# A hybrid decoder layer on one core: the second norm's gain moved from w_up's columns to the rows, and its row factor moved up in GpSimd's order

## The chip, the cores and the metric

One Trainium2 chip, of which the program uses one core. TensorE (PE) multiplies and transposes; VectorE (DVE), ScalarE (ACT) and GpSimd (POOL) do the elementwise work; SyncE (SP) issues the transfers. Each engine runs its own instructions in the order in which they stand, and an instruction that waits holds everything behind it on that engine. The metric is the device time of one execution in microseconds.

## The reference

One layer on 1024 tokens with 16 learned rows in front of them; width 1024, hidden width 4096, everything in float32.

```python
h = concatenate([meta, x])
hn = rms_norm(h, norm1_gain)
q, k, v, u = split(hn @ w_in)
h = h + concatenate([diff_attention(q, k, v, ...), conformer_conv(u, ...)]) @ w_out
hn = rms_norm(h, norm2_gain)
a = relu(hn @ w_up)
h = h + (a * a) @ w_down
return h[n_meta:]

def rms_norm(x, g):
    return x * rsqrt(mean(x * x) + EPS) * g
```

The change concerns the second `rms_norm` and what feeds `hn @ w_up`.

## The kernel before

**Numbers.** Every float32 operand of a product is held as a high and a low part, and each product is three matmuls (`three`: high by high at line 319, high by low at 320, low by high at 321). A pair is made by `halves` (lines 806 to 809): ACT copies the high part (L808), DVE or POOL subtracts it for the low part (L809).

**Stages.** First norm, input projection and convolution run to about 225 us; then keys, queries, values and attention, with `w_out`'s products mixed in, to about 475; then the second norm and the first products of `w_up`; the up-projection to about 824; the down-projection to the end.

**Second norm.** `attn_out(t, nh)` adds half a row tile of attention's result to the convolution's (L693, DVE) and squares it on ACT with the sums kept (`ssq`, L695). When both halves of a tile are there, two small POOL instructions make the factor `rs2` of its 128 rows (L698 `ms`, L699 the power, shown as `rs`). `normed(t)` multiplies the rows by it (L832, `xn`, two instructions per row tile), PE transposes them (L835, `htr`), and `norm_first` (tiles 7 to 4, read back from DRAM as `h2t`), `norm_second` (tiles 3 to 0, kept in SBUF as `h2k`) and `norm_third` make the operands from the transposed tiles. The last row tile is t = 0. The norm's gain is not in `xn`: it is multiplied into w_up's rows.

**Up-projection.** It is done in 16 groups of 256 columns by Strassen and Winograd's scheme of seven products; `up_product(g, n)` is one of them. Products 1 to 3 use rows as they are (`hn`), products 4 to 7 use sums of them (`hnt`: "t4", "t1", "t2", "t3"). `wload` fetches half of a group's columns into one of four buffers `wr` (L890) and scales it by the gain: for the early groups, in tiles of 128 columns, in one POOL instruction (L892); for all others in four ACT instructions per tile (L894). `up_prep` then makes the sums `s1`, `s2` on DVE and the pairs `wp`. `up_early` does products 1 and 2 of groups 0 to 3 as soon as the rows are there. In a later group, product 6 adds to product 1 in the same PSUM tile `px`, and ACT snaps the result into `sn` (L941) before product 7 may add to `px`.

**Order.** Nothing of the order is written by hand but a few marks: a list scheduler with simulated times sets each engine's order, and `tc.high_priority()` lifts what stands under it. Buffers come from pools: 4 of `wr` (which `h2t` uses too), 6 of `wp`, 7 of `ut` (`h2k`), 6 PSUM banks that `po`, `htr`, `px`, `py`, `pz` and `pw` share.

**Start.** SP loads the first rows, weights and small vectors one after the other; the convolution's taps `cw` are among them (L223), and `gains` [128, 2, 8] holds both norms' gains with the channel on the partition.

Of the kernel before, what the change touches and what calls it, by code (L numbers as in the profile page):

```python
# [16 lines left out]
P = 128  # L17
# [42 lines left out]
def hybrid_layer_kernel(  # L60
# [36 lines left out]
    def small(shape, name, bufs=2):  # L97
        return sp.tile(shape, F32, tag=name, name=name, bufs=bufs)
# [59 lines left out]

    xm = cp.tile([P, 8, 48], F32R, tag="xm", name="xm")
    G.memset(xm.bitcast(F32), 0.0)
    mraw = slot([NMETA, D], F32, "mraw")
    nc.sync.dma_start(mraw, meta)
# [62 lines left out]
    V.tensor_scalar(lnh[:, 1, :], cvec[:, :, 2], 0.5, None, ALU.mult)  # L227
    gsub = cp.tile([P, 1], F32, tag="gsub", name="gsub")
    V.tensor_scalar(gsub, cvec[:, 0, 3:4], (1.0 - 0.2) * P ** 0.5, None, ALU.mult)

    gq = tmp([P, HD], F32, "gq")
    gk = tmp([P, HD], F32, "gk")
# [451 lines left out]
    def attn_out(pool, t, nh, keep=None):  # L684

        if keep is None:
            hs = tmp([P, 512], F32, "hs")
        else:
            hs = keep.tile([P, 512], F32, tag="ut", name="h2k", bufs=UT)
            h2t.setdefault(t, []).append(hs)  # L690
        nc.sync.dma_start(hs, cvo[t, nh])
        ps = half_out(pool, ma, state[0, nh], t)
        V.tensor_tensor(out=hs, in0=hs, in1=ps, op=ALU.add)  # L693
        nc.sync.dma_start(h2d[t][:, 512 * nh:512 * nh + 512], hs)
        S.activation(ps, hs, AF.Square, scale=D ** -0.5, accum_out=ssq[:, t, nh:nh + 1])  # L695
        if nh:
            ms = small([P, 8], "ms", 4)[:, :1]
            G.tensor_scalar(ms, ssq[:, t, 0:1], ssq[:, t, 1:2], EPS, ALU.add, ALU.add)  # L698
            G.tensor_tensor(out=rs2[:, t:t + 1], in0=ms, in1=mhalf[:, :1], op=ALU.pow)  # L699

    uqs, pend = [], []
    for t in range(NT):
# [48 lines left out]
    for n in range(-1, len(units) + BLAG):  # L751
        if n < 0:
            with tc.high_priority(offset=PRI):
                for f, *a in fill_at.get(n, []):
                    f(*a)
            continue
        if n != 1:
            ahead(n)
        if n == 0 and APOSN[1] >= NT:
            for j in range(4):  # L760
                conv_act(1, j)
        if n < len(units):
            mixed.append(mix(*units[n], *pend.pop(0)))
        if n == 1:
            st_pool.__exit__(None, None, None)
            yt_pool.__exit__(None, None, None)
            aux_pool = tc.tile_pool(name="aux", bufs=1, side="right", reuse_waits="tile")
            aux = aux_pool.__enter__()
            ap2 = tc.tile_pool(name="ap2", bufs=2, reuse_waits="tile")
            late_pools["pt"] = ap2.__enter__()  # L770
            ahead(1)
        if n >= BLAG:
            i, h = units[n - BLAG]
            values(i, h, mixed.pop(0))
            if h == NH - 1:
                done.append((n + FIN, i, state["osb"], state["oss"]))
            if done and (n >= done[0][0] or n - BLAG == len(units) - 1):
                finish(*done.pop(0)[1:])
        with tc.high_priority(offset=PRI):
            for f, *a in fill_at.get(n, []):  # L780
                f(*a)
# [39 lines left out]
    def normed(t):  # L821

        if t in h2t:
            hv = h2t[t]
        else:
            h2 = up.tile([P, D], F32, tag="wr", name="h2t", bufs=WRB)
            nc.sync.dma_start(h2, h2d[t])
            hv = h2[:, :512], h2[:, 512:]
        banks = []
        for kf in range(2):  # L830
            xn = sp.tile([P, 512], F32, tag="raw", name="xn", bufs=4)
            V.tensor_scalar(xn, hv[kf], rs2[:, t:t + 1], None, ALU.mult)  # L832
            bank = pcm.tile([P, 4, P], F32, tag="mm", name="htr")
            for q in range(4):
                T.transpose(bank[:, q, :], xn[:, q * P:(q + 1) * P], ident)  # L835
            banks.append(bank)
        return banks
# [29 lines left out]
    def norm_third():  # L867

        for name in ("t4", "t1", "t3"):
            operand(name)  # L870
            for c in (256, 0):
# [3 lines left out]
                if name == "t4":  # L875
                    sub(V, r21, t2, r21)
                    halves(hi, lo, r21)
                elif name == "t1":
                    halves(hi, lo, t1)
                else:  # L880
                    sub(V, t2, t2, r11)
                    halves(hi, lo, t2)
# [4 lines left out]
    def wload(g, j, n):  # L887

        r = up.tile([P, 4, n], F32, tag="wr", name="wr", bufs=WRB, padded_shape=[P, 4, 256])
        nc.sync.dma_start(r, w_up[512 * j:512 * j + 512, 256 * g:256 * g + n].rearrange("(k p) f -> p k f", p=P))  # L890
        if n == P:
            G.tensor_tensor(out=r, in0=r, in1=gains[:, 1, 4 * j:4 * j + 4].unsqueeze(2).broadcast_to([P, 4, P]), op=ALU.mult)  # L892
        for k in range(4) if n > P else ():
            S.activation(r[:, k, :], r[:, k, :], AF.Copy, scale=gains[:, 1, 4 * j + k:4 * j + k + 1])  # L894
        return r

    def wpair(g, n, v, eng=None):
# [199 lines left out]
            next(run[g])  # L1097
    next(run[NG - 1])
    up_pool.__exit__(None, None, None)
    ps_c.__exit__(None, None, None)  # L1100
    tr_pool.__exit__(None, None, None)

# [134 lines left out]
```

## Time and profile before

| | |
|---|---|
| median of 3 runs | 1135.59 us (1133.06 to 1140.71) |
| profiled execution | 1135.33 us, of which 1133.2 is the traced span |
| PE busy | 1098.8 us, 97% of the span |
| DVE, ACT, POOL busy | 817.2, 617.1 and 149.2 us |
| mean granted clock of PE | 0.995 of full speed |

A busy share is an average over stages. An engine at 97% leaves some 34 us in which it waited; whether another engine's work matters is read at those waits. A granted clock of 1.00 is PE's full 2.4 GHz, 0.50 its lower level of 1.2 GHz.

### The profile page before, as it was taken

How to read it: one execution, taken by the hardware profiler on the slowest of the kernel's cores; microseconds unless marked ns; L12 is line 12 of the kernel's file. 1: busy time of each engine (PE TensorE's matmuls, PEld its weight loads, DVE VectorE, ACT ScalarE, POOL GpSimd, SP SyncE). 2: the span in 40 equal slices, each digit the busy share in tenths (PEclk: the TensorE clock that was granted, in tenths of full speed). 3: DMA queues.
4: the chain of work that ended last, by engine and by line, in shares of the span. 5: the costliest groups of instructions: out<-in, count | busy, mean ns of one | idle time of the engine just before them, and what ended most of it. 6: DMA issues, size and time to landing. Idle time of an engine off the chain costs nothing.

```text
span 1133.2 us, 15762 instructions
## 1 busy us (share of the span) xinstructions
PE 1098.8 (97%) x5696; PEld 925.5 (82%) x5696; DVE 817.2 (72%) x1354; ACT 617.1 (54%) x1378; POOL 149.2 (13%) x160
## 2 busy tenths in 40 slices
PE   6999999999999999898999999999999999999998
PEld 6999788877788887786888877888878888888887
DVE  7699899977888788689688868787656545356340
ACT  7521465447667677568767667767555333323320
POOL 3000564313001351261000000000000000000000
PEclk9999999999999999998999999999999999999999
DMA  7420011100213411365489989879399675565600
GB/s 266 121 76 1 1 38 38 29 10 19 75 66 103 131 66 66 122 224 170 154 309 330 323 277 343 320 251 339 125 336 380 251 258 212 197 227 201 221 38 37
DMA packets 89309, 191.23 MB, mean 169 GB/s; under 512 B 7552, under 2 KB 28288, under 8 KB 83600
## 3 DMA queue, kind: packets, MB, share of 16 engines
q1 hardware_dynamic: 89232, 190.24, 48.0%
q8 instruction: 44, 0.72, 0.3%
q14 instruction: 33, 0.27, 0.1%
HBM read 130.44 MB, written 59.77 MB: 168 GB/s over the span
## 4 chain that ended last, share of the span: by engine, by line
PE 72%; DVE 10%; DMA 8%; ACT 5%; issue 3%; POOL 1%; SPq 0%; DVEq 0%; ACTq 0%; POOLq 0%
PE py L319 6%; PE py L320 6%; PE py L321 6%; PE px L321 5%; PE px L319 5%; PE px L320 5%; DMA wr<-in_w_up 3%; PE pu L319 3%; PE pu L320 3%; PE pu L321 3%; DMA wdr<-in_w_down 3%; PE pq L320 3%; PE pq L319 3%; PE pq L321 3%; PE ops L620 2%
## 5 line engine op out<-in xcount | busy, mean ns | idle before, releaser
L809 DVE TENSOR_TENSOR pair<-rv,pair 128x2048 fp32r<-128x2048 f32 x56 | 127.0, 2289 | 112.0 <-ACT pair L808 111.8
L808 ACT ACTIVATE pair<-rv 128x2048 fp32r<-128x2048 f32 x56 | 105.2, 1911 | 163.2 <-PE py L321 77.9
L319 PE MATMUL py<-pair 128*128 128x512 f32 x256 | 99.6, 389 | 0.0
L320 PE MATMUL py<-pair 128*128 128x512 f32 x256 | 99.6, 389 | 0.0
L321 PE MATMUL py<-pair 128*128 128x512 f32 x256 | 99.6, 389 | 0.0
L319 PE MATMUL px<-pair 128*128 128x512 f32 x192 | 74.8, 390 | 1.0 <-ACT pair L808 1.0
L320 PE MATMUL px<-pair 128*128 128x512 f32 x192 | 74.7, 389 | 0.0
L321 PE MATMUL px<-pair 128*128 128x512 f32 x192 | 73.8, 390 | 0.2 <-DVE pair L809 0.2
L320 PE MATMUL pu<-xT,w 128*128 128x260 f32 x256 | 72.4, 286 | 0.0
L321 PE MATMUL pu<-xT,w 128*128 128x260 f32 x256 | 71.7, 285 | 0.0
L319 PE MATMUL pu<-xT,w 128*128 128x260 f32 x256 | 71.7, 286 | 0.0
L894 ACT ACTIVATE wr<-wr,gains 128x256 f32<-128x256 f32 x128 | 55.0, 498 | 30.6 <-DMA wr<-in_w_up 29.7
L945 ACT ACTIVATE a<-a 128x512 f32<-128x512 f32 x60 | 36.9, 626 | 35.9 <-DVE a L812 24.6
L321 PEld LDWEIGHTS py<-pair 128*128 128x128 f32 x256 | 48.1, 188 | 10.0
L319 PEld LDWEIGHTS py<-pair 128*128 128x128 f32 x256 | 48.1, 188 | 9.9
L320 PEld LDWEIGHTS py<-pair 128*128 128x128 f32 x256 | 48.1, 188 | 9.9
L319 PE MATMUL px<-hnt,wp 128*128 128x512 f32 x128 | 50.5, 395 | 3.9 <-ACT sn L941 3.9
L321 PE MATMUL pq<-w,xT 128*128 128x512 f32 x128 | 50.9, 398 | 0.0
L319 PE MATMUL pq<-w,xT 128*128 128x512 f32 x128 | 50.9, 397 | 0.0
L320 PE MATMUL pq<-w,xT 128*128 128x512 f32 x128 | 50.8, 397 | 0.0
L320 PE MATMUL px<-hnt,wp 128*128 128x512 f32 x128 | 50.4, 394 | 0.4 <-DVE hnt L809 0.4
L321 PE MATMUL px<-hnt,wp 128*128 128x512 f32 x128 | 50.5, 394 | 0.0
(301 smaller groups left out, 3197.6 us busy)
## 6 DMA issues: line engine op xcount, KB each, us to landing
rv<-as SPq DMA_DIRECT2D x28, 1024.0 KB, 6.3
wr<-in_w_up SPq DMA_DIRECT2D x32, 512.0 KB, 5.2
as<-a SPq DMA_DIRECT2D x64, 256.0 KB, 5.4
wdr<-in_w_down SPq DMA_DIRECT2D x8, 2048.0 KB, 9.5
ws<-wdr SPq DMA_DIRECT2D x32, 512.0 KB, 4.5
rv<-ws SPq DMA_DIRECT2D x16, 1024.0 KB, 4.8
as<-as SPq DMA_DIRECT2D x48, 256.0 KB, 4.1
rv<-in_w_down SPq DMA_DIRECT2D x12, 1024.0 KB, 6.6
```

What stands on the lines that cost most here:

```text
L319: T.matmul(ps, st[0], mv[0], start=first, stop=False, skip_group_check=more)
L320: T.matmul(ps, st[0], mv[1], start=False, stop=False, skip_group_check=more)
L321: T.matmul(ps, st[1], mv[0], start=False, stop=last, skip_group_check=more)
L620: T.matmul(ops, u[:, 0, b, :], vb.rearrange("p a e -> p (a e)"), start=b == 0, stop=False)
L808: S.activation(hi, src, AF.Copy)
L809: (eng or V).tensor_tensor(out=lo, in0=src, in1=hi.bitcast(F32), op=ALU.subtract)
L894: S.activation(r[:, k, :], r[:, k, :], AF.Copy, scale=gains[:, 1, 4 * j + k:4 * j + k + 1])
L945: S.activation(c, c, AF.Relu)
```

## The change

**Gain.** `wload` no longer scales: the POOL multiply (L892) and the four ACT scales per tile (L894) are gone. In their place `xn` is made by one instruction that multiplies the rows by their factor and by the gain, which must then lie along the row: `gain2` is a tile [128, 1024] with the gain repeated on every partition. It comes by two transfers: one at the start writes the 1024 gains into a row `grow` in DRAM, 4 bytes each, behind the taps on SP; one within attention broadcasts that row to all partitions (512 KB). Its space is found by moving `xm` to another pool.

**Order.** The two POOL instructions of `rs2` are marked high priority. The low parts of operand "t1" in `norm_third` go to POOL.

```diff
-    xm = cp.tile([P, 8, 48], F32R, tag="xm", name="xm")
+    xm = wpool[0].tile([P, 8, 48], F32R, tag="xm", name="xm", bufs=1)
...
+    grow = dr.tile([8, P], F32, tag="grow", name="grow")
+    nc.sync.dma_start(grow.rearrange("k p -> p k"), gains[:, 1, :])
...
         if nh:
-            ms = small([P, 8], "ms", 4)[:, :1]
-            G.tensor_scalar(ms, ssq[:, t, 0:1], ssq[:, t, 1:2], EPS, ALU.add, ALU.add)
-            G.tensor_tensor(out=rs2[:, t:t + 1], in0=ms, in1=mhalf[:, :1], op=ALU.pow)
+            with tc.high_priority():
+                ms = small([P, 8], "ms", 4)[:, :1]
+                G.tensor_scalar(ms, ssq[:, t, 0:1], ssq[:, t, 1:2], EPS, ALU.add, ALU.add)
+                G.tensor_tensor(out=rs2[:, t:t + 1], in0=ms, in1=mhalf[:, :1], op=ALU.pow)
...
+            gain_pool = tc.tile_pool(name="gain", bufs=1, side="right", reuse_waits="tile")
+            gain2 = gain_pool.__enter__().tile([P, D], F32, tag="gain2", name="gain2")
+            nc.sync.dma_start(gain2, grow.rearrange("k p -> (k p)").partition_broadcast(P))
...
-            V.tensor_scalar(xn, hv[kf], rs2[:, t:t + 1], None, ALU.mult)
+            V.scalar_tensor_tensor(xn, hv[kf], rs2[:, t:t + 1], gain2[:, 512 * kf:512 * kf + 512], ALU.mult, ALU.mult)
...
-                    halves(hi, lo, t1)
+                    halves(hi, lo, t1, G)
...
-        if n == P:
-            G.tensor_tensor(out=r, in0=r, in1=gains[:, 1, 4 * j:4 * j + 4].unsqueeze(2).broadcast_to([P, 4, P]), op=ALU.mult)
-        for k in range(4) if n > P else ():
-            S.activation(r[:, k, :], r[:, k, :], AF.Copy, scale=gains[:, 1, 4 * j + k:4 * j + k + 1])
```

In the new kernel the lines behind the additions have moved: the low part is L817, `xn` L840, the rows' factor L703 and L704, the squares L699, `sn` L945, the load of `wr` L898.

The order of POOL from the low parts of the first early tiles on, before; the lines with `rs` are the factors of row tiles 1 and 0:

```order
L809 TENSOR_TENSOR wp<-wr,wp 128x512 x4
L698 TENSOR_SCALAR ms<-ssq 128x1
L892 TENSOR_TENSOR wr<-wr,gains 128x4x128 x2
L699 TENSOR_TENSOR rs_2665<-ms,mhalf 128x1
L892 TENSOR_TENSOR wr<-wr,gains 128x4x128 x2
L809 TENSOR_TENSOR wp<-wr,wp 128x512 x2
L698 TENSOR_SCALAR ms<-ssq 128x1
L809 TENSOR_TENSOR wp<-wr,wp 128x512
L699 TENSOR_TENSOR rs_2665<-ms,mhalf 128x1
L809 TENSOR_TENSOR wp<-wr,wp 128x512
```

And now; the first `rs` is row tile 2's, and the two that follow each other behind the four `wp` are those of tiles 1 and 0:

```order
L817 TENSOR_TENSOR wp<-wr,wp 128x512 x2
L703 TENSOR_SCALAR ms<-ssq 128x1
L704 TENSOR_TENSOR rs_2667<-ms,mhalf 128x1
L817 TENSOR_TENSOR wp<-wr,wp 128x512 x4
L703 TENSOR_SCALAR ms<-ssq 128x1
L704 TENSOR_TENSOR rs_2667<-ms,mhalf 128x1
L703 TENSOR_SCALAR ms<-ssq 128x1
L704 TENSOR_TENSOR rs_2667<-ms,mhalf 128x1
L817 TENSOR_TENSOR wp<-wr,wp 128x512 x2
L817 TENSOR_TENSOR hnt_6502<-scr,hnt_6502 128x4x256 x2
```

The multiplies of `wr` are gone, both last factors stand together ahead of the last two `wp`, and operand "t1"'s low parts (`hnt`) stand at the end.

The order of DVE from row tile 1's last sum to row tile 0's `xn`, before:

```order
L693 TENSOR_TENSOR h2k<-h2k,po 128x512
L832 TENSOR_SCALAR xn<-h2k,rs_2665 128x512 x2
L812 TENSOR_TENSOR scr<-htr,hraw 128x4x128
L812 TENSOR_TENSOR scr<-htr,scr 128x4x128
L812 TENSOR_TENSOR hraw<-scr,hraw 128x4x256
L809 TENSOR_TENSOR hnt_6195<-scr,hnt_6195 128x4x128
L809 TENSOR_TENSOR hn_6196<-htr,hn_6196 128x4x128
L812 TENSOR_TENSOR scr<-scr,hraw 128x4x256
L812 TENSOR_TENSOR scr<-htr,hraw 128x4x128
L832 TENSOR_SCALAR xn<-h2k,rs_2665 128x512 x2
```

And now, from row tile 1's `xn` to the release of its PSUM banks:

```order
L840 SCALAR_TENSOR_TENSOR xn<-h2k,rs_2667,gain_3418 128x512 x2
L697 TENSOR_TENSOR h2k<-h2k,po 128x512
L823 TENSOR_TENSOR s_6367<-wr 128x512
L820 TENSOR_TENSOR s_6368<-s_6367,wr 128x512
L820 TENSOR_TENSOR wr<-wr 128x4x128
L820 TENSOR_TENSOR scr<-htr,hraw 128x4x128
L840 SCALAR_TENSOR_TENSOR xn<-h2k,rs_2667,gain_3418 128x512 x2
L820 TENSOR_TENSOR scr<-htr,scr 128x4x128
L820 TENSOR_TENSOR hraw<-scr,hraw 128x4x256
L817 TENSOR_TENSOR hnt_6198<-scr,hnt_6198 128x4x128
L820 TENSOR_TENSOR scr<-htr,hraw 128x4x128
L817 TENSOR_TENSOR hn_6199<-htr,hn_6199 128x4x128
```

Three instructions that read a full group's `wr` (`s`, `s`, `wr`) now stand ahead of row tile 0's `xn`, and four that read row tile 1's transposed tiles (`scr`, `hnt`, `hn`) and a sum (`hraw`) have come to stand behind it.

The order of ACT around `sn` in the group of the stall near 683 us, before; L894 are the scales:

```order
L945 ACTIVATE a_7755<-a_7755 128x512
L808 ACTIVATE wp<-wr 128x512
L946 ACTIVATE a_7755<-a_7755 128x512
L945 ACTIVATE a_7771<-a_7771 128x512
L946 ACTIVATE a_7771<-a_7771 128x512
L894 ACTIVATE wr<-wr,gains 128x256 x2
L941 ACTIVATE sn<-px 128x512
L808 ACTIVATE wp<-wr 128x512
L894 ACTIVATE wr<-wr,gains 128x256 x2
```

And now, around the same `sn` (L945):

```order
L949 ACTIVATE a_7682<-a_7682 128x512
L950 ACTIVATE a_7682<-a_7682 128x512
L816 ACTIVATE wp<-wr 128x512
L949 ACTIVATE a_7698<-a_7698 128x512
L950 ACTIVATE a_7698<-a_7698 128x512
L945 ACTIVATE sn<-px 128x512
L816 ACTIVATE wp<-wr 128x512
L816 ACTIVATE wp<-s_7741 128x512
```

The scales are gone, and the first pair of the next group's weights (`wp<-wr`, the third row) reads the loaded tile itself.

The order of ACT where row tile 2's first half is squared (`po,ssq<-h2k`), before:

```order
L808 ACTIVATE hn_6022<-htr 128x4x128
L695 ACTIVATE po,ssq<-h2k 128x512
L849 ACTIVATE hraw<-htr 128x4x128
L808 ACTIVATE hn_6018<-htr 128x4x128
L695 ACTIVATE po,ssq<-h2k 128x512
L849 ACTIVATE hraw<-htr 128x4x128
L808 ACTIVATE hn_6022<-htr 128x4x128
L808 ACTIVATE wp<-wr 128x512
```

And now:

```order
L816 ACTIVATE hn_6029<-htr 128x4x128
L816 ACTIVATE wp<-wr 128x512
L857 ACTIVATE hraw<-htr 128x4x128
L816 ACTIVATE hn_6025<-htr 128x4x128
L699 ACTIVATE po,ssq<-h2k 128x512
L857 ACTIVATE hraw<-htr 128x4x128
```

The first early pair, `wp<-wr`, has come from behind the squares of both halves to stand ahead of the first, and it waits for its load alone.

## Rows read from the trace of the kernel before

**Rows 1.** The page: busy time of each engine, and DMA share in 40 slices.

```profile
PE 1098.8 (97%) x5696; PEld 925.5 (82%) x5696; DVE 817.2 (72%) x1354; ACT 617.1 (54%) x1378; POOL 149.2 (13%) x160
...
DMA  7420011100213411365489989879399675565600
```

**Rows 2.** Waits of PE: engine line waited for, us in all, times, longest.

```profile
PE htr L835 <- DVE xn L832: 4.7, 2, 4.4
PE px L319 <- ACT sn L941: 3.9, 2, 2.8
```

**Rows 3.** Windows of PE: us, busy (x), PEclk, DMA share, GB/s.

```profile
515.00:520.00 5.00, 3.95 (x14) 0.50 0.73 226
```

**Rows 4.** Timeline of PE around the first stall: start us, us, ..., idle before and releaser.

```profile
516.05 1.94 PE L835 MATMUL htr<-ident,xn 128*128 128x128 f32 x8 [4.41 <-DVE xn L832]
517.64 0.78 PE L319 MATMUL px<-hn,wp 128*128 128x512 f32 x1
...
520.95 0.39 PE L321 MATMUL px<-hn,wp 128*128 128x512 f32 x1
```

**Rows 5.** Timeline of PE around the second stall.

```profile
683.21 0.50 PE L319 MATMUL px<-hnt,wp 128*128 128x512 f32 x1 [2.79 <-ACT sn L941]
...
688.12 0.39 PE L321 MATMUL px<-hn,wp 128*128 128x512 f32 x1
688.35 0.39 PE L319 MATMUL px<-hn,wp 128*128 128x512 f32 x1
```

**Rows 6.** Timeline of ACT from 656 to 684 us.

```profile
657.80 1.71 ACT L894 ACTIVATE wr<-wr,gains 128x256 f32<-128x256 f32 x4 [1.77 <-DMA wr<-in_w_up]
...
678.21 0.61 ACT L808 ACTIVATE wp<-wr 128x512 fp32r<-128x512 f32 x1
...
681.77 0.91 ACT L894 ACTIVATE wr<-wr,gains 128x256 f32<-128x256 f32 x2 [1.24 <-DMA wr<-in_w_up]
682.59 0.57 ACT L941 ACTIVATE sn<-px 128x512 f32<-128x512 f32 x1
```

**Rows 7.** The page's costliest groups: the scale of w_up on ACT.

```profile
L894 ACT ACTIVATE wr<-wr,gains 128x256 f32<-128x256 f32 x128 | 55.0, 498 | 30.6 <-DMA wr<-in_w_up 29.7
```

**Rows 8.** Timeline of DVE from 499 to 529 us.

```profile
504.93 2.44 DVE L832 TENSOR_SCALAR xn<-h2k,rs 128x512 f32<-128x512 f32 x2 [1.03 <-POOL rs L699]
...
508.80 2.06 DVE L812 TENSOR_TENSOR hraw<-scr,hraw 128x1024 f32<-128x1024 f32 x1
...
514.49 1.81 DVE L832 TENSOR_SCALAR xn<-h2k,rs 128x512 f32<-128x512 f32 x2
...
522.09 1.21 DVE L812 TENSOR_TENSOR hraw<-scr,hraw 128x1024 f32<-128x1024 f32 x1
```

**Rows 9.** Timeline of POOL from 486 to 524 us.

```profile
489.66 1.15 POOL L892 TENSOR_TENSOR wr<-wr,gains 128x512 f32<-128x512 f32 x1 [7.06 <-PE htr L835]
...
496.14 5.41 POOL L809 TENSOR_TENSOR wp<-wr,wp 128x512 fp32r<-128x512 f32 x4
...
504.34 0.55 POOL L699 TENSOR_TENSOR rs<-ms,mhalf 128x1 f32<-128x1 f32 x1
...
512.85 1.54 POOL L699 TENSOR_TENSOR rs<-ms,mhalf 128x1 f32<-128x1 f32 x1
```

**Rows 10.** Line 832 by itself: duration ns min/median/max, first and last start.

```profile
L832 DVE TENSOR_SCALAR xn<-h2t,rs x8: 477/480/486, 479.3 to 486.3; 128x512 f32<-128x512 f32 x8
```

**Rows 11.** The same view of line 644.

```profile
L644 DVE SCALAR_TENSOR_TENSOR ma<-otr,gsub,ma x8: 742/749/752, 347.0 to 482.1; 128x512 fp32r<-128x512 f32 x8
```

**Rows 12.** Timeline of PE at 487 to 490 us.

```profile
487.64 1.91 PE L835 MATMUL htr<-ident,xn 128*128 128x128 f32 x16
489.30 0.48 PE L319 MATMUL po<-wo,ma 128*128 128x512 f32 x1
```

**Rows 13.** The page's DMA issues: count, KB each, median us from issue to landing.

```profile
wr<-in_w_up SPq DMA_DIRECT2D x32, 512.0 KB, 5.2
```

**Rows 14.** DMA from 19 to 23 us: packets, MB, share of 16 engines.

```profile
q1 hardware_dynamic: 644, 0.37, 42.1%
```

More of the change, by code (lines that the diff above doesn't have):

```diff
@@ L1099, in hybrid_layer_kernel @@
     up_pool.__exit__(None, None, None)
+    gain_pool.__exit__(None, None, None)
     ps_c.__exit__(None, None, None)
```

## The prediction

> **What bounds the kernel now.** The page comes first: PE is busy 1098.8 of 1133.2 us [rows 1], so a change that leaves PE's own work alone can only win some of the other 34 us, or lose by making PE wait anew. The waits of PE say whose they are. Two entries belong to work that this change touches: `htr` waited 4.7 us for `xn` on DVE, 4.4 of it once, and `px` waited 3.9 us for `sn` on ACT, twice, 2.8 at the longest [rows 2]. The rest is at the start, in attention and at the end. The windows then show what a stall costs afterwards: in the 5 us around the end of the first, the granted clock is 0.50, which is 1.2 GHz of 2.4 [rows 3]. The timelines of PE give the price. Call the first stall A. It is 4.41 us long; the eight transposes behind it then take 1.59 us, from 516.05 to 517.64, where sixteen took 1.66 at full clock [rows 4, 12], so 0.76 us are lost; the next eight matmuls take 3.31 us, to 520.95, where the full-clock pitch of 0.23 us (688.12 to 688.35) gives 1.84, so 1.5 us are lost [rows 4, 5]. A is worth 4.4 + 0.8 + 1.5 = 6.7 us. Call the waits for `sn` B: 3.9 us, and behind the longer one fourteen matmuls took 4.91 us in place of 3.2, another 1.7 [rows 2, 5]: 5.6 us. A and B together, 12.3 us, are 1.1% of the time and all that this change can win.
>
> **The scales on ACT (B).** Removed are 128 ACT instructions of 498 ns, 55.0 us of busy time, and 29.7 us in which ACT stood still in front of them for w_up's loads [rows 7]. ACT is busy 54%, so the sum is worth nothing by itself; it counts only where `sn` stands behind it. There it does: at 657.80 and at 681.77 ACT had waited 1.77 and 1.24 us for a load, scaled, and only then made `sn` (at 682.59), while PE had been idle since 680.42 [rows 5, 6]. In the new order nothing in front of this `sn` waits for a load that was asked for just before: the pair ahead of it reads a tile of the next group, and that group's pair was made at 678.21, while the scale of its tile began at 657.80 [rows 6], so the load has some 20 us of slack where it had none. I take B as gone: -5.6 us. Its bounds are 0, if the relu and square of `a` that still stand in front are late too, and -5.6.
>
> **The factor and the gain in `xn` (A).** Three things move. First, the POOL multiplies go and `rs` comes sooner: at 504.34 and 512.85 us before, the latter in 1.54 us [rows 9]. By the new order only six low parts of 1.35 us (5.41 for four) stand ahead of the last two factors, which then depend on their squares. Second, `xn` takes a second tensor: the nearest row is 749 ns for a scalar-tensor-tensor of that size against 480 ns for the old form with POOL quiet [rows 10, 11]; 16 times 0.27 is 4.3 us of DVE in all, of which 0.5 us stand in front of the last transposes. Against that, with POOL busy the old pair took 2.44 us, not 0.96 [rows 8, 10], and POOL will be quieter. Third, order. Row tile 1's `xn` should start at about 503.3 (DVE waited for `rs` until 504.93, for 1.03 us [rows 8], and one sum of 0.6 us now stands behind instead of ahead) and end at about 504.8. Then comes one sum of 0.6 us, and then the three instructions on `wr`, which wait for a full group's loads. I put these at about 506: six low parts of 1.35 us from about 491 on end at 499, and later if ACT hands over the last of them late; I take 500.5, and a full group's load lands 5.2 us after its issue [rows 13]. Three at 0.6 us and one more put row tile 0's `xn` at 508.7 to 510.1, in time for PE, which asked for it at 511.64 (516.05 less 4.41).
>
> But A doesn't go whole. In the new order the second half of row tile 0's transposes takes a PSUM bank that a later DVE instruction frees (`scr<-htr`, then `hn<-htr`), five instructions behind that `xn`: 3 times 0.6 and 1.2 for the sum, 3 to 4 us. So the matmuls behind the transposes start at 513.7 to 515, not at 512.7, and this is compared with 517.64 and the half clock behind it.
>
> **The new wait on ACT.** The other order of ACT adds one. The first early pair stands ahead of the square of row tile 2's first half, and PE's next product into that bank needs the square. In the kernel before, the load landed by 489.66, where POOL had been idle for 7.06 us [rows 9], and PE went on at 489.30 without a wait [rows 12]. Now: landed at 489.7 to 490.3, pair 0.6, two copies of 0.5, square 0.6, so PE goes on at about 492.3: 3 us of stall, 0 at best if the load is early, and up to 2.3 more if the clock falls as it did behind A. Part of it is not additional: a PE that is 3 us later at row tile 0's transposes finds the banks free. Either way the matmuls behind the transposes start at about 515. Against 517.64 that is 2.6 us, with 1.5 us of half clock on top where the clock holds: 2.6 to 4.1, and I take -3.5. The bounds are 0 and -6.7.
>
> **T1's low parts.** DVE loses two instructions of 1.21 us, POOL gets two of twice the 1.35 us of a half-sized one [rows 8, 9], 2.7 each; their reader on PE comes after some 110 matmuls of 0.23 us [rows 5], 25 us behind the transposes. Covered, so 0; if that cover were gone it would cost up to 2.7.
> What POOL does beside DVE has a price that a row shows: the same 128x1024 difference took 2.06 us with POOL busy throughout and 1.21 with POOL idle [rows 8, 9], 0.85 lost in 2.06. The Trainium skill (SBUF — State Buffer, "Who interferes with whom") states more: a DVE instruction with two SBUF inputs and a GpSimd instruction that reads SBUF exclude each other, and the second waits until the first has ended. By that rule the two low parts would hold DVE for up to 5.4 us while its operands for PE are due, and A's gain would be nothing, 1131 us in all; the row shows a slowing by less than the whole of POOL's instruction, and I keep to the row.
>
> **The two transfers.** `grow` is 1024 elements of 4 bytes at the start. Nearest row: 644 small packets took 42.1% of 16 queues in 4 us, so 42 ns each [rows 14]; 1024 of them hold all queues for 2.7 us, twice that if a 4-byte piece costs double. The queues are near full in the first slice (7 of 10 [rows 1]), and the last row tiles and weights come behind it. What they feed isn't used at once, so I take +1, with bounds 0 and +5. `gain2`'s 512 KB go in attention, where the DMA digits are 0 to 4 [rows 1]: 0.
>
> **Sum.** 1135.3 (the profiled execution, 0.3 below the median of the runs shown) - 5.6 - 3.5 + 1.0 = 1127.2, say 1127.5 us.
>
> **Rivals.**
> *Both stalls go whole.* The load at 489 is early, the banks are free in time, the start is covered: 1135.3 - 12.3 = 1123.0. For it: `xn` is ready before PE asks. Against it: the bank order above, and DVE is full in that stretch. 0.17.
> *New waits eat A, and the start adds.* The stall at 489 with its clock (3 + 2.3) takes A's place, `grow` costs 2 or more, or POOL's two low parts of 2.7 us hold DVE outright, or DVE waits longer for the group's loads: 1135.3 - 5.6 + 0 to 5, so 1130 to 1135. For it: each of these instructions now stands behind a load with no slack. 0.24. That the factor is no sooner after all, because its squares stand on ACT behind pairs that wait for loads, ends here too.
> *Slower.* One mechanism: the first pair of a group waits for its load on ACT, in front of `sn`, in the up-projection, as the scale did. It decides if loads land over 20 us later than now. DMA is busiest there, at digits of 7 to 9 from 567 to 793 us [rows 1]; if four groups each stalled PE as at 683, by 4.5 us, that is +18, less B's 5.6: 1147.7. Against it: the slack of 20 us. 0.06.
> The forecast has 0.53.
>
> **How the numbers follow.** A measurement of this kernel can tell some 1%, 11.4 us, from no change. Faster by more means below 1124.2: the first rival and a small tail of the forecast, 0.2. Slower by more means above 1146.9: the third rival, 0.06. Within: 0.74. The range for 8 in 10 reaches from 1122, a little below the full gain, to 1135.5, the end of the second rival; outside are the third, and what none of them foresees.
>
> **What would show it.** Right: no L892 or L894; no wait of `px` for `sn`; the wait of `htr` for `xn` at 516 gone, with a wait of 1 to 3 us for the banks (DVE `scr` or `hn`) or for ACT's square near 489 in its place; granted clock 1.00 at 685 to 690; `xn` at 0.75 us. Wrong: a wait of PE for `sn` that stays although no scale is there; PE's first product of the input projection later than before; or a new wait in the up-projection behind `wp`.

## The result, and the profile after

| | kernel before | changed kernel |
|---|---|---|
| median of 11 runs each | 1134.31 us (1131.94 to 1140.71) | 1141.27 us (1138.09 to 1145.5) |
| ratio, 95% interval | | 1.0062 [1.0045, 1.0079] |
| span of the profiled execution | 1133.2 us | 1138.9 us |

The changed kernel is slower by 0.6%, 7 us. The forecast of 1127.5 us and its range, 1122 to 1135.5, were both wrong, and the sign with them, though the size stays within 1%.

The page after, the line that answers to the first of [rows 1]. ACT alone has changed by much: it lost 47 us of busy time, and PE has as little time to spare as before.

```profile
PE 1101.0 (97%) x5696; PEld 926.5 (81%) x5696; DVE 820.3 (72%) x1352; ACT 569.9 (50%) x1250; POOL 144.2 (13%) x154
```

The waits of PE after, in the columns of [rows 2]:

```profile
PE xtr L190 <- DVE xs L185: 3.7, 1, 3.7
PE px L323 <- ACT sn L945: 3.3, 2, 2.1
PE px L323 <- ACT wp L816: 2.5, 1, 2.5
...
PE htr L843 <- DVE scr L820: 1.9, 1, 1.9
```

Both entries that the forecast counted on have shrunk or moved. The 4.4 us for `xn` are gone, `scr` holds 1.9 in their place. `sn` still costs 3.3 us. Two entries are new: 3.7 at the start, 2.5 for `wp`. Where they lie is told by the timeline of PE after:

```profile
18.36 1.97 PE L190 MATMUL xtr<-ident,xs 128*128 128x128 f32 x8 [3.68 <-DVE xs L185]
...
520.70 0.66 PE L843 MATMUL htr<-ident,xn 128*128 128x128 f32 x4 [1.86 <-DVE scr L820]
...
534.01 0.50 PE L323 MATMUL px<-hnt,wp 128*128 128x512 f32 x1 [2.45 <-ACT wp L816]
...
764.75 0.50 PE L323 MATMUL px<-hnt,wp 128*128 128x512 f32 x1 [2.13 <-ACT sn L945]
...
785.33 0.50 PE L323 MATMUL px<-hnt,wp 128*128 128x512 f32 x1 [1.21 <-ACT sn L945]
```

Windows of PE after (columns of [rows 3]): the clock falls behind `scr` and behind `wp`, and from 600 to 700 us, where the stalls for `sn` of [rows 5] stood, PE is never idle.

```profile
520.00:525.00 5.00, 4.30 (x14) 0.70 0.50 171
...
535.00:540.00 5.00, 5.00 (x15) 0.66 0.59 213
...
600.00:700.00 100.00, 100.00 (x443) 1.00 0.94 325
700.00:840.00 140.00, 136.54 (x599) 1.00 0.73 256
```

In the kernel before the same windows read 96.05 of 100 and 138.82 of 140: PE won 4.0 us in the one and lost 2.3 in the other. Along PE the changed kernel is 3.8 us behind at the first product of the input projection (19.98 against 16.14), 5.2 behind at the first transposes of the second norm (485.1 against 479.8) and 5.6 behind at the last product (1134.3 against 1128.7). So in these two traces the loss is there before the second norm begins (3.8 us at the start, 1.4 up to 480, where the granted clock was 0.91 from 280 to 300 us; such a dip stands elsewhere in other executions, 0.94 from 400 to 480 us in that of the kernel with both parts undone below), and the stretches of A and B together come out at nothing.

**The start.** `grow` is issued at 7.66 us. DMA from 12 to 16 us before, and from 11 to 12 and from 12 to 16 us after:

```profile
DMA packets 452, 1.65 MB, mean 414 GB/s; under 512 B 48, under 2 KB 48, under 8 KB 452
...
DMA packets 1088, 0.28 MB, mean 275 GB/s; under 512 B 1037, under 2 KB 1037, under 8 KB 1088
...
DMA packets 386, 0.45 MB, mean 113 GB/s; under 512 B 277, under 2 KB 277, under 8 KB 386
```

Most of the 1024 pieces pass between 11 and 12 us (1037 packets under 512 bytes, 288 in that time before). What is slow is what comes behind them: in the 4 us that follow, the queues move 0.45 MB where they moved 1.65 before. The four loads of rows that are issued from 8.66 us on land after 12.2 us in the median and not 7.0, and PE's transposes of them wait.

**DVE beside POOL.** The timeline of DVE after, around the transposes and in the up-projection:

```profile
505.22 0.68 DVE L820 TENSOR_TENSOR scr<-htr,hraw 128x512 f32<-128x512 f32 x1
...
512.67 0.69 DVE L823 TENSOR_TENSOR s<-wr 128x512 f32<-128x512 f32 x1 [1.47 <-DMA wr<-in_w_up]
513.39 1.67 DVE L820 TENSOR_TENSOR s<-s,wr 128x512 f32<-128x512 f32 x1
...
516.18 1.40 DVE L840 SCALAR_TENSOR_TENSOR xn<-h2k,rs,gain 128x512 f32<-128x512 f32 x2
...
522.29 3.40 DVE L817 TENSOR_TENSOR hnt<-hraw,hnt 128x1024 fp32r<-128x1024 f32 x1
528.62 2.80 DVE L817 TENSOR_TENSOR hnt<-scr,hnt 128x512 fp32r<-128x512 f32 x1
...
761.60 0.69 DVE L823 TENSOR_TENSOR s<-wr 128x512 f32<-128x512 f32 x1 [3.68 <-DMA wr<-in_w_up]
762.21 0.68 DVE L823 TENSOR_TENSOR a<-sn,pw 128x512 f32<-128x512 f32 x1
...
777.57 1.22 DVE L820 TENSOR_TENSOR wdr<-wdr 128x1024 f32<-128x1024 f32 x1 [5.96 <-DMA wdr<-in_w_down]
```

And of POOL after; the last two are the low parts of "t1" that the change put there:

```profile
501.16 5.95 POOL L817 TENSOR_TENSOR wp<-wr,wp 128x512 fp32r<-128x512 f32 x4
...
507.59 0.91 POOL L704 TENSOR_TENSOR rs<-ms,mhalf 128x1 f32<-128x1 f32 x1
512.05 0.30 POOL L703 TENSOR_SCALAR ms<-ssq 128x1 f32<-128x1 f32 x1 [3.55 <-ACT po L699]
512.43 0.56 POOL L704 TENSOR_TENSOR rs<-ms,mhalf 128x1 f32<-128x1 f32 x1
...
521.83 2.79 POOL L817 TENSOR_TENSOR hnt<-scr,hnt 128x1024 fp32r<-128x1024 f32 x1 [0.61 <-ACT hnt L816]
528.47 2.40 POOL L817 TENSOR_TENSOR hnt<-scr,hnt 128x1024 fp32r<-128x1024 f32 x1 [3.86 <-ACT hnt L816]
```

The ends are to be compared, not the durations. POOL's first ends at 524.62 and DVE's difference beside it at 525.69, 1.07 us later; the second ends at 530.87 and DVE's at 531.42, 0.55 later. A quiet one takes 1.21 [rows 8] and 0.68. So DVE did next to nothing until POOL had ended, and then its own work. An instruction that reads one of its two inputs from a PSUM tile (`scr<-htr,hraw` at 505.22) keeps its 0.68, though it lies wholly beside POOL's four low parts from 501.16 to 507.11.

**`sn`.** ACT after, at the two stalls:

```profile
762.92 0.63 ACT L949 ACTIVATE a<-a 128x512 f32<-128x512 f32 x1 [4.01 <-DVE a L823]
...
764.12 0.58 ACT L945 ACTIVATE sn<-px 128x512 f32<-128x512 f32 x1
...
781.16 0.63 ACT L949 ACTIVATE a<-a 128x512 f32<-128x512 f32 x1 [6.93 <-DVE a L823]
...
784.70 0.58 ACT L945 ACTIVATE sn<-px 128x512 f32<-128x512 f32 x1
```

ACT waits no longer for a load, but for DVE's sum `a`, and that stands on DVE behind the two instructions above that wait for loads, 3.68 us for w_up and 5.96 for w_down. The waits of DVE and ACT after, in all, times, longest:

```profile
DVE wdr L820 <- DMA wdr<-in_w_down: 21.4, 8, 6.0
DVE s L823 <- DMA wr<-in_w_up: 12.9, 9, 3.7
ACT wp L816 <- DMA wr<-in_w_up: 4.5, 2, 3.2
```

Before, ACT's scales waited 29.7 us for w_up's loads [rows 7], DVE 12.6 for w_down's and for w_up's never long enough to be listed.

### The profile page after: what moved, and what is told of

It reads as the page before. It is cut to its first block, busy times and chain, and to the rows that moved or that the text cites. A ratio compares the mean times of both kernels' runs of the same rounds, so it can differ in the third digit from the quotient of the medians.

```text
span 1138.9 us, 15620 instructions
## 1 busy us (share of the span) xinstructions
PE 1101.0 (97%) x5696; PEld 926.5 (81%) x5696; DVE 820.3 (72%) x1352; ACT 569.9 (50%) x1250; POOL 144.2 (13%) x154
## 4 chain that ended last, share of the span: by engine, by line
PE 81%; DVE 6%; DMA 6%; ACT 4%; POOL 2%; issue 1%; SPq 0%; POOLq 0%; DVEq 0%; ACTq 0%
PE px L325 7%; PE px L323 7%; PE px L324 7%; PE py L324 6%; PE py L323 6%; PE py L325 6%; PE pu L323 3%; PE pu L325 3%; PE pu L324 3%; PE pq L323 3%; PE pq L324 3%; PE pq L325 3%; DMA wr<-in_w_up 2%; PE ops L624 2%; PE pw L324 2%; PE pw L323 2%
## 5 line engine op out<-in xcount | busy, mean ns | idle before, releaser
L817 DVE TENSOR_TENSOR pair<-rv,pair 128x2048 fp32r<-128x2048 f32 x56 | 127.0, 2289 | 112.9 <-ACT pair L816 112.8
L323 PE MATMUL px<-hnt,wp 128*128 128x512 f32 x128 | 50.3, 393 | 5.9 <-ACT sn L945 3.3
L816 ACT ACTIVATE wp<-wr 128x512 fp32r<-128x512 f32 x64 | 39.9, 628 | 30.0 <-PE pw L325 17.8
L820 DVE TENSOR_TENSOR wdr<-wdr 128x1024 f32<-128x1024 f32 x32 | 39.0, 1219 | 21.5 <-DMA wdr<-in_w_down 21.4
L324 PE MATMUL px<-hnt,wp 128*128 128x512 f32 x128 | 49.8, 389 | 0.0
```

What stands on the lines that cost most here:

```text
L323: T.matmul(ps, st[0], mv[0], start=first, stop=False, skip_group_check=more)
L324: T.matmul(ps, st[0], mv[1], start=False, stop=False, skip_group_check=more)
L816: S.activation(hi, src, AF.Copy)
L817: (eng or V).tensor_tensor(out=lo, in0=src, in1=hi.bitcast(F32), op=ALU.subtract)
L820: eng.tensor_tensor(out=out, in0=a, in1=b, op=ALU.subtract)
```

## The experiments

Ratios are to the kernel before in the same set of runs, with 95% intervals. The difference of two ratios from different sets is good to some 0.0025. The theory at the outset: the start (3.5 to 4.5 us) and the low parts on POOL (1 to 3) undo what A and B give. The rivals: the new order costs it, or B was never there.

**Only `grow`**, in the kernel before.

```diff
+    grow = dr.tile([8, P], F32, tag="grow", name="grow")
+    nc.sync.dma_start(grow.rearrange("k p -> p k"), gains[:, 1, :])
```

> The kernel before with one thing added: the transfer of 1024 elements of 4 bytes into a DRAM row at the start, which nothing reads. Theory 1 (the pieces hold the queues, and the rows of x behind them come late): PE's first product of the input projection starts near 20.0 us in place of 16.1, nothing later gives that back, and the time is 3.5 to 4.5 us above the kernel before. Rival (the start of the changed kernel is late for its other order of transposes, or the loss is made good in attention): the first product near 16.1, or the time within 1.5 us of the kernel before.

Measured: 1.0049 [1.0032, 1.0067], 5.6 us for one transfer of 4 KB that nothing reads, a little more than expected. PE in its timeline:

```profile
19.56 1.97 PE L190 MATMUL xtr<-ident,xs 128*128 128x128 f32 x8 [5.21 <-DVE xs L185]
21.18 1.22 PE L323 MATMUL pu<-xT,w 128*128 128x260 f32 x4
```

**The same 4 KB in 128 pieces** of 32 bytes, in the kernel before.

```diff
+    grow = dr.tile([P, 8], F32, tag="grow", name="grow")
+    nc.sync.dma_start(grow, gains[:, 1, :])
```

> The kernel before with the same 4 KB written to DRAM at the start, but in 128 pieces of 32 bytes in place of 1024 of 4. Theory 1 in its narrow form (the price is the number of pieces): an eighth of the other's, PE's first product at 16.1 to 16.8 us, time within 1 us of the kernel before. Rival (a small write at the start costs by itself, or the order that the scheduler makes around it does): first product at 19 us or later, 3 us or more above.

Measured: 1.0011 [0.9996, 1.0026], the first product at 16.09 us. DMA from 12 to 16 us:

```profile
DMA packets 471, 1.68 MB, mean 420 GB/s; under 512 B 61, under 2 KB 61, under 8 KB 471
```

With the 1024 pieces of the run before it was 92 GB/s. Nor is SP's own time the price: the next rows are issued at 8.31 us here and at 8.38 there. So the same bytes in fewer and longer pieces cost nothing measurable. Number and length changed together; no run tells which of them is paid.

**`grow` in attention**, in the changed kernel: the transfer from a copy of the column, made after the convolution.

```diff
-    nc.sync.dma_start(grow.rearrange("k p -> p k"), gains[:, 1, :])
...
+            G.tensor_copy(gcol, gains[:, 1, :])
+            nc.sync.dma_start(grow.rearrange("k p -> p k"), gcol)
```

> The changed kernel with the 4-byte transfer moved from the start into attention, right ahead of the load that reads it; the 1024 gains are copied by GpSimd first, so that they cannot be sent earlier. Theory 1: first product back near 16.1 us, time 3.5 to 4.5 us below the changed kernel, some 1137 us, so still not faster than the kernel before. Rival (the start was not the price): less than 1.5 us below the changed kernel. If SP's queue, held by the transfer in attention, matters, PE waits anew between 280 and 300 us.

Measured: 1.0011 [0.9992, 1.0029], 0.0051 below the changed kernel, the amount that `grow` alone had added. The waits at 517, 530, 760 and 780 us stay (1.92, 2.43, 1.24, 1.07).

**"t1"'s low parts back on DVE**, in the changed kernel (`halves(hi, lo, t1)`).

> The changed kernel with operand t1's low parts back on DVE. Theory 2 (a GpSimd instruction that reads SBUF holds a DVE instruction with two SBUF inputs until it has ended): the two DVE instructions that took 3.40 and 2.80 us beside the low parts of 2.79 and 2.40 fall to 1.2 and 0.7, DVE gets two of 1.2 us back, its chain is some 2 us shorter, and PE's wait of 2.45 us for wp at 534 us shrinks to 1 us or less; time 1 to 3 us below the changed kernel. Rival (the prediction's reading, a slowing by less than half): the two fall by less than 1 us each, DVE's chain is longer by 1 us or more, and the wait grows.

Measured: 1.0016 [1.0002, 1.0031], 0.0046 below the changed kernel, more than the 1 to 3 us expected. DVE's timeline has the instruction of 3.40 us in 1.22 and that of 2.80 in 0.68; the low parts that came back take DVE 1.21 us each:

```profile
521.28 1.22 DVE L817 TENSOR_TENSOR hnt<-hraw,hnt 128x1024 fp32r<-128x1024 f32 x1
...
526.55 0.68 DVE L817 TENSOR_TENSOR hnt<-scr,hnt 128x512 fp32r<-128x512 f32 x1
```

PE's wait of 2.45 us for `wp` is gone, and one of 0.49 for `hnt` stands near it. The waits for `sn` are shorter too, 1.9 us and not 3.3.

**"t1"'s low parts on POOL, in the kernel before** (`halves(hi, lo, t1, G)`).

> The kernel before with operand t1's low parts on GpSimd, nothing else. Theory 2: a DVE instruction with two SBUF inputs that meets one of them takes its own time plus what is left of it, 2.5 to 3.5 us, and the time does not fall: 0 to 3 us above the kernel before. Rival (DVE is relieved by 2.4 us and slowed by less): DVE is ready for operand t2 some 2 us sooner, and the time is the same or 1 us lower, as PE waited only 0.4 us there.

Measured: 0.9988 [0.997, 1.0006]. The hold is there too: two `xn` on DVE take 3.91 us, while POOL works from 512.89 to 516.65, and PE waits for them for 4.59 us, 4.41 before. A row of DVE's timeline and one of POOL's:

```profile
513.02 3.91 DVE L832 TENSOR_SCALAR xn<-h2k,rs 128x512 f32<-128x512 f32 x2
...
512.89 2.34 POOL L809 TENSOR_TENSOR hnt<-scr,hnt 128x1024 fp32r<-128x1024 f32 x1
```

Nothing is lost in all. That doesn't show the hold to be free in this order: in this trace PE waits 5.6 us for `xn` (4.7 before) and 1.0 for a new `wp`, but only 1.0 for `sn` (3.9 before), so a loss at the transposes can be hidden by a gain in the up-projection.

**A write of zeros in place of the low parts**, in the changed kernel.

```diff
-                    halves(hi, lo, t1, G)
+                    S.activation(hi, t1, AF.Copy)
+                    G.memset(lo.bitcast(F32), 0.0)
```

> The changed kernel, but GpSimd writes zeros into the two low parts of operand t1 in place of the differences (the low parts of t1 are left out): GpSimd is busy at the same place, and reads nothing from SBUF. By the lock (only a GpSimd instruction that reads SBUF holds a DVE instruction with two SBUF inputs) DVE's instructions beside it go back from 3.40 and 2.80 us to about 1.2 and 0.7, PE's wait of 2.45 us for wp is gone, and the ratio falls from 1.006 to about 1.002 to 1.004. Rival (any GpSimd work beside DVE slows it): they stay above 1.5 times their quiet durations.

Measured: 1.0021 [1.0002, 1.004]. DVE in its timeline, and POOL in the next:

```profile
515.14 1.66 DVE L820 TENSOR_TENSOR s<-s,wr 128x512 f32<-128x512 f32 x1
516.73 0.68 DVE L820 TENSOR_TENSOR wr<-wr 128x512 f32<-128x512 f32 x1
```

```profile
514.79 1.47 POOL L817 TENSOR_TENSOR wp<-wr,wp 128x512 fp32r<-128x512 f32 x1
516.20 1.85 POOL L888 MEMSET hnt<- 128x1024 f32 x2
```

The same kind of DVE instruction, two inputs from SBUF, stands beside a POOL difference in the first row (1.66 us) and beside the memset in the second (0.68). In these rows not POOL's being busy, but its reading holds DVE.

**Both undone**, in the changed kernel: `grow` in attention, "t1" on DVE.

> The changed kernel with both parts undone that were found dear: the 4-byte transfer in attention, and operand t1's low parts on DVE. Theory (the two prices add up): 0.46% from the start and 0.46% from the low parts off the changed kernel, so 1131 to 1133 us, 2 to 4 us below the kernel before, the first product at 16 us, and PE's wait for wp near 530 us gone. Rival (the parts overlap, the wait at the row banks or for sn takes the gain): within 1.5 us of the kernel before.

Measured: 0.9978 [0.9961, 0.9994], 1130.26 against 1132.77 us. That is 0.0084 below the changed kernel, where the two steps alone took off 0.0051 and 0.0046, so the two prices add up within the noise. What is left is what the rest of the change, gain on the rows and no scales, is worth: 2.5 us of the 9.1 that A and B were to bring. PE still waits 1.74 us for `scr` and 1.25 and 1.97 us for `sn`.

**The kernel before without its scales** (lines 891 to 894 taken out, so the gain is left out).

> The kernel before without the scaling of w_up, on ACT and on GpSimd; the second norm's gain is left out of the computation, nothing is put in its place. It is the change without its own costs (no transfers, no second tensor in xn, low parts of t1 on DVE). By the prediction's steps for the two stalls: 5.6 and 3.5 us below the kernel before, 1125 to 1127 us. By what the changed kernel's trace showed (each stall comes back in another place: row banks, sn behind a relu): 0 to 4 us below, 1131 to 1135 us, with a wait of 1 to 2 us for scr near 517 and one for sn behind 700 us.

Measured: 0.9985 [0.9969, 1.0001]. Even with nothing put in their place the scales' 55 us of ACT are worth 0 to 3.5 us: PE waits 2.5 us for `sn` at other places (3.9 before) and 2.4 for `scr`.

**`a21`'s relu and square in one DVE instruction**, on top of both undone.

```diff
-        relu2(a21)
+        V.scalar_tensor_tensor(a21, a21, 0.0, a21, ALU.max, ALU.mult)
```

> The same kernel with one more edit: the relu and square of a21, two ACT instructions that stand in front of sn and wait for DVE, are one DVE instruction (maximum with 0, times itself). Theory 3 (sn is late because it stands on ACT behind these two, which wait for DVE's sum): PE's waits for sn near 760 and 780 us, 2 to 3.3 us together, are gone, time 2 to 4 us below the kernel with the two parts undone. Rival (DVE itself is late there, or the relu of a11 holds sn as well): the waits for sn stay at 1 us or more in all, time within 1 us.

Measured: 0.9965 [0.9948, 0.9982], which overlaps the interval of both undone. Of the two stalls for `sn` the one near 758 us is gone, the other, 1.91 us at 786, now comes behind the relus of `a12` and `a22` on ACT:

```profile
783.12 1.23 ACT L952 ACTIVATE a<-a 128x512 f32<-128x512 f32 x2 [7.01 <-DVE a L823]
...
785.81 0.58 ACT L948 ACTIVATE sn<-px 128x512 f32<-128x512 f32 x1
```

**The same without w_down's differences** on DVE.

```diff
-        sub(V, r11, r12, r11)
-        sub(V, r12, r22, r12)
-        sub(V, r22, r22, r11)
-        sub(V, r21, r22, r21)
```

> The kernel with both put back and a21's relu-square on DVE, with the four differences that DVE makes of each half of w_down left out (what is stored is the raw w_down). If DVE's wait for w_down's loads (17.6 us in all there) is what makes sn late through the sums of a, the wait of 1.9 us of PE for sn near 786 is gone and no wait above 0.7 us takes its place in the up-projection; the time falls by 2 to 4 us, a ratio of 0.993 to 0.995. Rival (the sums of w_up that DVE makes wait for w_up's loads, whatever w_down does): a wait of 1 to 2 us for sn stays, and the ratio stays at 0.995 to 0.998.

Measured: 0.994 [0.9916, 0.9963], which overlaps the interval with the differences. No wait of PE for `sn` is left, though DVE still waits 12.0 us for w_up's loads. That the differences are gone takes DVE's work away as well as its waits, so the run shows that they hold `sn`, and not by which of the two.

**The sums of the first full groups behind row tile 0's `xn`**, on top of a21's. The code of the sums stands later, and a tiny POOL copy makes them depend on `scr`.

```diff
     norm_second(0)
+    for p in preps:
+        next(p)
...
+        if g < 2:
+            G.tensor_copy(s1[:, 0, 0:1], scr[0][:, 0, 0, col(0):col(0) + 1])
```

> The kernel with both transfers and low parts put back and the relu-square of a21 on DVE, and one thing more: the sums that read the first two full groups' loads stand on DVE behind row tile 0's xn and the copies that free its PSUM banks. Theory (A was given back because those sums went in front of xn): PE's wait for scr behind the transposes (1.96 us there) falls below 0.7, and the time is 1 to 3 us below that kernel's ratio of 0.9965, so 0.994 to 0.996. Rival (the stretch is bound by the sum of DVE's work, not by its order): another wait of 1 to 3 us comes for the pairs made of those sums (wp, s), and the ratio stays at 0.996 to 0.998.

Measured: 0.9965 [0.9946, 0.9985], as without the step. What its trace was to show is read from a further run of the same kernel (1131.87 us against 1135.83, one execution each).

> The kernel with both put back, a21's relu-square on DVE and the sums behind row tile 0's xn (without the later differences of w_down), once more, for a trace at full clock. If the step did in this stretch what it does together with the later differences, the wait for scr behind row tile 0's transposes is below 0.7 us, and since its time was that of the kernel without the step, PE waits 1 to 3 us more at sn in the up-projection than the 1.9 us there. Rival: a wait for scr, hn or wp of 1 us or more stays at the transposes, and sn is as before.

The first of these came true. No wait for `scr`, `hn` or `wp` above 0.72 us is left between 500 and 540 us; in the up-projection the waits for `sn` went from 1.9 to 3.1 us:

```profile
689.14 0.51 PE L321 MATMUL px<-hnt,wp 128*128 128x512 f32 x1 [2.17 <-ACT sn L950]
```

and the clock is 0.91 in the 20 us around it. What the step won at the transposes was lost at `sn`.

**w_down's differences later**, on top of a21's, without the step on the sums. `one` comes from the next group's `a22` and is 1.

```diff
+        V.tensor_scalar(one, after[:, 0:1], 0.0, 1.0, ALU.mult, ALU.add)
-        sub(V, r11, r12, r11)
-        sub(V, r12, r22, r12)
+        V.scalar_tensor_tensor(r11, r12, one, r11, ALU.mult, ALU.subtract)
+        V.scalar_tensor_tensor(r12, r22, one, r12, ALU.mult, ALU.subtract)
```

> The kernel with both put back and a21's relu-square on DVE, whole, with the differences of w_down made to wait for the next group's a22 (the first two as a scalar-tensor-tensor with a factor that comes from a22 and is 1), so that DVE does not stand before them while the load is on its way. If DVE's wait for w_down is what remains of the stalls at sn, most of what the kernel without these differences won comes back without leaving work out: PE's wait for sn in the up-projection below 0.7 us, DVE's wait for w_down's loads from 17.6 us to under 5, ratio 0.994 to 0.996. Rival (the later differences push other work of DVE, or the later stores the next load, into PE's way): a wait of over 1 us of PE for another product's operand in the up-projection, ratio 0.9965 to 1.000.

Measured: 1.0017 [1.0002, 1.0032], worse than without the step, and neither theory as written: DVE's wait for w_down didn't fall (22.4 us), and it is again `sn` that PE waits for, five times, 6.1 us in all.

**Both of these steps together.**

> The same, and the sums that read the first two full groups' loads behind row tile 0's xn and the copies that free its banks. If the bank wait of 1.9 us behind row tile 0's transposes is those sums' doing, PE's wait for scr there falls below 0.7 us and the ratio is 0.001 to 0.002 below the kernel without this step. Rival (the stretch holds as much work of DVE in either order): a wait of the same size for a pair (wp) or a low part (hnt) comes behind it, and the ratio is the same within 0.001.

Measured: 1125.75 us against 1134.25, 0.9926 [0.9907, 0.9945], the fastest of all, and 0.0091 below the kernel without the step on the sums, where 0.001 to 0.002 were expected. PE between 500 and 540 us, and from 600 to 700:

```profile
500.00:540.00 40.00, 39.20 (x182) 1.00 0.52 170
600.00:700.00 100.00, 100.00 (x443) 1.00 0.91 321
```

Before, PE was busy for 35.15 us of the first window at a clock of 0.91. The longest wait there is 0.72 us, and none for `sn` is left. The waits of A and B are gone here, and the time is 8.5 us below the kernel before, not the 12.3 at which the two were priced; one wait that has nothing to do with them, for `pair` at 826 us, is 2.3 us long and not 1.0. DVE still waits 15.2 us for w_down's loads, so the sum of its waits doesn't decide. That it is decided by whether a sum of `a` stands behind such a wait when ACT's next `sn` is due fits the rows, but was not tested by itself.

## Why the prediction was wrong, point by point

**The start: "I take +1", mis-sized.** It measured 5 to 6 us. The sum took the 2.7 us for which 1024 pieces at 42 ns hold the queues [rows 14] as the whole price, and 1 us of it as what PE would feel. The pieces themselves were mostly through within a microsecond; the loads behind them ran at 113 GB/s where they had run at 414, and PE's first product came 3.8 us late in this trace and 5.0 with `grow` alone. Why loads are so slow behind these pieces, no run shows. Wrong, too, was the reason for taking less, "What they feed isn't used at once". The rows that are issued behind `grow` feed the last transposes ahead of the first product, and in the kernel before PE went from these, at 12.19 us, to that product, at 16.14, without a pause. The value lay at the upper bound of +5 or a little beyond. The Trainium skill (DMA: Bandwidth & Descriptors, "Specifications") puts line rate at 512 bytes and more; pieces of 4 and of 32 bytes are both below that, and 128 of the latter cost nothing measurable, so being below it doesn't make the price by itself.

**T1's low parts: "Covered, so 0" and "I keep to the row", wrong.** They cost 0.0046, 5 us. The cover of 25 us was worked out for POOL's own result, and held. What it didn't cover is DVE, held for 2.2 and 2.1 us in front of the sums and low parts that PE's next pairs need. The row was misread. The instruction of 2.06 us [rows 8] ran from 508.80 to 510.86; the second of the POOL low parts beside it ended at 509.77:

```profile
507.05 2.72 POOL L809 TENSOR_TENSOR wp<-wr,wp 128x512 fp32r<-128x512 f32 x2
```

So DVE was done 1.09 us later. That is as good as the 1.07 of the trace after, so the row showed a full hold, not a slowing. The rule that was weighed and set aside, the Trainium skill's (SBUF — State Buffer, "Who interferes with whom") that a DVE instruction with two SBUF inputs and a GpSimd instruction that reads SBUF exclude each other, agrees with every pair of rows shown here, and its half on GpSimd instructions that only write agrees with the memset. By the prediction's own estimate for this rule the forecast would have been 1131; with the start at +5 as well, 1135.

**B: "nothing in front of this `sn` waits for a load that was asked for just before", wrong.** The 20 us of slack hold for ACT's pair, which was the only reader looked at. The scales had been the first readers of a group's load. With them gone, DVE's `s<-wr` is the first, and DVE waits (12.9 us after). ACT's relu takes `a` from DVE, and stands in front of `sn`. So the wait went from ACT to DVE and came back to `sn` one engine later: 5.6 us expected, 3.3 of 3.9 us of stalls still there, elsewhere. Only the half clock behind the stalls was won whole in this trace (1.00 from 600 to 840 us), so B brought some 2.3 us. The rows show this chain for the stall at 764.75, and the run with a21's relu on DVE, where that one is gone, bears it out. The stall at 785.33 is another: the load that DVE waits for there is w_down's, which never was scaled. DVE's waits for these loads grew from 12.6 to 21.4 us, and to 23.1 in the kernel before without its scales, so they grow with the scales' removal; by which way is open. The lower bound named ("if the relu and square of `a` ... are late too") was the case, without its cause.

**A: the mechanism right, the sum too good.** The stall of 4.41 us went, and the wait for the banks came, 1.86 us where 1 to 3 were said. The whole stretch begins 5.2 us late, which is to be taken off its times: `rs`, at 512.43, was 5.7 us sooner than the 512.85 of before [rows 9], as the mechanism has it, and row tile 0's `xn`, at 516.18, 0.8 to 2.2 us later than the 508.7 to 510.1 that were said. It stood behind the sums on `wr`, which waited 1.47 us for their load and ran 1.67 beside POOL. With "t1" on DVE and `grow` late PE still waited 1.74 us there; with the sums behind `xn`, nothing above 0.72.

**The wait on ACT near 489: there, and cheap.** ACT stood 3.25 us in front of the pair. PE lost 0.4 us by it, not 3, and no clock.

**The mark of high priority moved nothing.** Put into the kernel before, or taken from the changed one, it leaves every engine's order as it is. That the factors stand earlier on POOL comes from the multiplies being gone.

**The rivals.** The second one named most of the right mechanisms (the start 2 or more, POOL's low parts that "hold DVE outright", longer waits for loads), but as alternatives that eat A, each at 0 to 5 us; all came at once, and A's own size could not pay for them. The slower rival, loads 20 us late on ACT, didn't happen.

**Still open.** Why the two last steps, each worth nothing or less, are worth 0.4% together: each also moves the scheduler's order in all later groups, and which of these moves frees `sn` wasn't tried apart. Nor is it shown how much of the 2.5 us that the change is worth without its two prices belongs to A and how much to B.

## What to carry to other kernels

When an instruction that waits for a load is removed, look for the next reader of that load: the wait moves there, and what stands behind that reader on its engine is the new cost. Before work goes to POOL, compare where its instructions and DVE's neighbours end, not how long they take; a DVE instruction that ends its own quiet duration after POOL's was held, and it is DVE's queue that pays. A small transfer is to be counted in pieces (here 1024 of 4 bytes against 128 of 32), and at a kernel's start it is paid by the loads that are issued behind it, not by its own time.

## What the runs showed of the hardware

- 1024 pieces of 4 bytes cost 5.6 us at the start, 128 pieces of 32 bytes 1.3 us with an interval that holds 0. Behind the former the queues moved 92 and 113 GB/s from 12 to 16 us, behind the latter 420, and 414 without either.
- The hold between DVE and POOL also meets DVE's `xn` as a tensor-scalar, which has one tensor input: two of them take 3.91 us beside POOL and 0.96 quiet [rows 10]. The Trainium skill's section (SBUF — State Buffer, "Who interferes with whom") names tensor_scalar among those that can take the shared ports; the trace agrees.
- It goes both ways: POOL's `ms` of 128x1 takes 0.30 us alone and 1.67 from 508.38 in the kernel before with "t1" on POOL, while DVE's `hraw<-scr,hraw` of 128x1024 runs until 509.36.
- After a stall for `sn` the granted clock falls in some executions and not in others: 0.91 around 689 us with 2.17 us of wait, 1.00 from 700 to 840 after stalls of 2.13 and 1.21.
